# A two-layer trunk on one core: another order of the first stage, the embedding in two parts, and clipped differences on ScalarE

## Chip, core and metric

The kernel runs on one core of one Trainium2 chip. The metric is device microseconds from launch to end, the median of several executions. Engine names below: TensorE (PE, with PEld for its weight loads), VectorE (DVE), ScalarE (ACT), GpSimd (POOL), SyncE (SP).

## The reference

Two layers over a sequence of 512 rows of width 1024, all in fp32. Layer 0 mixes by a state-space scan (SSD, 8 groups of 4 heads, chunks of 128 rows), layer 1 by a gated MLP with a masked spatial product; each is followed by a SwiGLU FFN and a gated embedding.

```
for i in range(2):
    hn = rmsnorm(h, norm_mix[i])
    h = h + (ssd_mixer(hn, ...) if i % 2 == 0 else gmlp_mixer(hn, ...))
    h = h + swiglu(rmsnorm(h, norm_ffn[i]), ffn_w_gate[i], ffn_w_up[i], ffn_w_down[i])
    e = rmsnorm(p[i] @ ple_w_proj[i], ple_norm[i])
    gate = sigmoid(rmsnorm(h, ple_gate_norm[i]) @ ple_w_gate[i])
    h = h + gate * e
return rmsnorm(h, final_norm)
# inside the scan, per group and chunk:
lmat = exp(segsum(da))              # exp(cs[l] - cs[s]) where l >= s, else 0
y = einsum(C, B, lmat, x * dt) + C . previous states * exp(cs)
```

## The kernel before

The program holds the rows of `h` transposed, as 8 tiles `H[k]` of 128 features by 512 rows. Each weight arrives in raw tiles of 1 MB (two buffers) on SyncE's queue. A unit of 128x1024 is split in a high part `whi` (ScalarE, L88) and a low part `wlo` (VectorE, L89), three buffers each, and each product is three fp32r matmuls (`mm3`, L282 to L284): high by high, high by low, low by high. Activations are split likewise (`split`, L287 and L288).

The **first stage** (L663 to L728) is kept in the order of the code on every engine: sums of squares of the four row chunks of `x`, transposes, the row factors `rs0` (L421), scaled and split tiles of X (L426 to L430), and the products of the first two weight units (B and C of group 0). After it come two transposes of parameters (`to_columns`, L381), the product `wdt` · `H` (L737, 16 records) that gives dt, its copy (L738), and from it dt, the sums `cs` and their exponentials.

Everything after that is ordered by a scheduler that goes by code order and priorities; each engine then runs a fixed list. The **scan** of a group (`ssd(g)`) is a generator, advanced by `tock` while the projections of later groups run. It loads the rows of `cs` from DRAM (`csb`), takes clipped differences `min(cs[l] - cs[s], 0)` (L545, four per chunk) and their exponential (L546), forms `cb` (L585), its masked copy `cbm` (L587), `xdt` (L602), multiplies `csb` by `cbm` (L610, four), then states (L617) and outputs (L561, L563). Last come squares of the gated output `sq` and the group's statistic (`stat`: ScalarE's high part L287, VectorE's low part `rs` L288, matmuls L296 and L297, square root, reciprocal). The statistic of group g−1 falls among the steps of group g. There are two `sq` and two `rs` buffers.

After the last output projection stands the embedding of `p` (`ple_embed`, 48 matmuls), then the remainder of the output projection, each block of which is normalised (`nf.block`, L450 and L451), then the FFN. The FFN's own statistic keeps one `rs` buffer until the FFN ends. During it `spatial()` prepares the second layer: masked transposes `wsT`, and column sums, a fp32 matmul of `ones` with each (L935, 8 records), used by L938.

Of the kernel before, what the change touches and what calls it, by code (L numbers as in the profile page):

```python
# [43 lines left out]
class Weights:  # L44
# [16 lines left out]

    def _load(self, r):
        while self.loaded <= min(r, len(self.raws) - 1):
            raw = self.raw_pool.tile([P, 2048], F32, tag="wraw", name=f"wraw{self.loaded}")
            for dst, src in self.raws[self.loaded][0]:
                self.nc.sync.dma_start(out=dst(raw), in_=src)
            self.raws[self.loaded][1] = raw
            self.loaded += 1
# [33 lines left out]
def trunk(ctx: ExitStack, tc: tile.TileContext, x, p, norm_mix, norm_ffn, ssd_w_in, ssd_conv_w,  # L102
# [99 lines left out]
    add_proj(0)  # L202
    add_rows(ssd_w_out[0], 14, 2)
    add_ffn(0)
    for m in range(4):
# [32 lines left out]
    for c in range(NCH):  # L238
# [3 lines left out]
        x_tok.append((a, b))  # L242
    W._load(1)

# [87 lines left out]

    def ple_embed(i, spare):
        (ph, pl) = zip(*spare)
        E, accum = [], None
        for m2 in range(2):
            (wh, wl), = W.get()
            for mi in range(4):
                m = m2 * 4 + mi
                ps = bank()  # L340
                for k in range(2):
                    mm3(ps, wh[:, k, mi * P : (mi + 1) * P], wl[:, k, mi * P : (mi + 1) * P], ph[k], pl[k], k == 0, k == 1)
                e = slot(f"e{m}")
                nc.vector.tensor_scalar_mul(e, ps, pcol(80 + i * 8 + m))
                if accum is None:
                    accum = work("cbm")
                    act(accum, ps, AF.Square, scale=1.0 / 32)
                else:
                    sq = work("sq")
                    act(sq, ps, AF.Square, scale=1.0 / 32)  # L350
                    nc.gpsimd.tensor_tensor(accum, accum, sq, op=ALU.add)
                E.append(e)
# [6 lines left out]

        return E, finish()  # L360

# [40 lines left out]

    def x_rms(c):
        tt(ss[:, c : c + 1], ss2[:, c, 0:1], ss2[:, c, 1:2], op=ALU.add)
        act(rtok[:, c], ss[:, c : c + 1], AF.Sqrt, bias=eps6)
# [7 lines left out]

    rows = [None]

    def x_rows(c0, c1):
        if c0 == 0:
            rows[0] = bank()
        for c in range(c0, c1):
            tr(rows[0][:, c * P : (c + 1) * P], rtok[:, c].to_broadcast([P, P]))  # L420
        nc.vector.tensor_copy(rs0[:, c0 * P : c1 * P], rows[0][:, c0 * P : c1 * P])  # L421

# [103 lines left out]
    def ssd(g):  # L526
# [14 lines left out]
        def seg(c):  # L541

            for hh in range(4):
                o = lm[c][:, hh * P : (hh + 1) * P]
                nc.vector.tensor_scalar(o, o, cs[:, c, 4 * g + hh : 4 * g + hh + 1], 0.0, op0=ALU.subtract, op1=ALU.min)  # L545
            act(lm[c], lm[c], AF.Exp)  # L546

# [115 lines left out]
    with in_order(tc):  # L663
        warm(8)
        to_columns(3, rowN, 16)
        x_sums(0)
        x_transpose(0, 0, 6)
        x_sums(1)
        x_rms(0)
        x_transpose(1, 0, 6)  # L670
        x_sums(2)
        x_rms(1)
        x_transpose(2, 0, 6)
        x_sums(3)
        x_rms(2)
        x_rows(0, 3)
        x_transpose(3, 0, 6)
        x_rms(3)
        warm(2)
        x_rows(3, 4)  # L680
        warm(8)
        unit_hi(0)
# [4 lines left out]
        products(0, 0)  # L687
        x_lo(1, V_)
        products(0, 1)
        unit_hi(1)  # L690
# [24 lines left out]
        x_lo(7, G_)  # L715
        x_keep(3)
        W.taken = 2
        W._split(2)
        for k in range(4, KD):
            x_keep(k)  # L720
            products(0, k)
            products(1, k)
        nc.vector.tensor_copy(rowB[96:112].rearrange("b (h e) -> b h e", e=64),
                              d2[96:112].unsqueeze(2).to_broadcast([16, 2, 64]))
        to_columns(0, rowA, P)
        to_columns(1, rowB, P)

        tt(wdt, wdt, pcols[:, 3, :KD].unsqueeze(2).to_broadcast([P, KD, 32]), op=ALU.mult)  # L728
    for m in range(2):
        bc(m, first[m])  # L730
    dtT = work("csb")
    alog = dtT[:, :32]

    ps = bank()
    for k in range(2):
        for j in range(4):
            mm(ps[j * 32 : (j + 1) * 32], wdt[:, 2 * j + k], H[2 * j + k], start=k == 0, stop=k == 1)  # L737
    nc.vector.tensor_copy(dtT, ps)  # L738
    ps_dt = bank()
# [106 lines left out]
    while running:  # L846
        tick()
    E, finish_e = ple_embed(0, spare)
    assert not running


    nf = Norm(lambda k: pcol(16 + k))
    for m2 in range(2):
# [6 lines left out]
        for mi, ps in enumerate(pss):  # L860
            add_h(4 * m2 + mi, ps)
            nf.block(4 * m2 + mi)


# [57 lines left out]
    def spatial():  # L922
# [9 lines left out]
        yield  # L932
        for j in range(4):
            ps = bank()
            mm(ps, ones, wsT[j], start=True, stop=True)  # L935
            for gg in range(4):
# [127 lines left out]
    ffn(nf1, npg1.block, embed())  # L1064
    h_tok = [[slot(f"xh{2 * c + nt}") for nt in range(2)] for c in range(NCH)]

# [26 lines left out]
    def norm_out(c0, c1):  # L1093
        rms_tok(rtf, 1, c0, c1)
        for c in range(c0, c1):
            for n in range(2):
                o = slot(f"xl{2 * c + n}")
                if n and c == 3:
# [5 lines left out]
    for nt in range(2):  # L1104
# [19 lines left out]
        if nt == 0:  # L1124
            rtok2 = rstd_tok(npg1.accum)
            transpose_h(0)
            transpose_h(1)
        us = W.get(4 - first) if nt else []
# [41 lines left out]
```

## Time and profile before

| | |
|---|---|
| time, median of 3 | 1577.62 us (1577.13 to 1578.09) |
| the profiled execution | 1578.97 us |
| its span | 1577.0 us |
| mean granted TensorE clock | 0.997 |
| TensorE busy | 1553.9 us, 99% |
| VectorE, ScalarE, GpSimd busy | 904.9, 642.3, 285.7 us |

The span runs from the first to the last instruction; the execution's own time adds what lies around it. In the rows further down a record gives the start, the duration, the engine, the line, what it writes and reads, and in brackets how long the engine stood idle before it and what ended that.

### The profile page before, as it was taken

How to read it: one execution, taken by the hardware profiler on the slowest of the kernel's cores; microseconds unless marked ns; L12 is line 12 of the kernel's file. 1: busy time of each engine (PE TensorE's matmuls, PEld its weight loads, DVE VectorE, ACT ScalarE, POOL GpSimd, SP SyncE). 2: the span in 40 equal slices, each digit the busy share in tenths (PEclk: the TensorE clock that was granted, in tenths of full speed). 3: DMA queues.
4: the chain of work that ended last, by engine and by line, in shares of the span. 5: the costliest groups of instructions: out<-in, count | busy, mean ns of one | idle time of the engine just before them, and what ended most of it. 6: DMA issues, size and time to landing. Idle time of an engine off the chain costs nothing.

```text
span 1577.0 us, 18227 instructions
## 1 busy us (share of the span) xinstructions
PE 1553.9 (99%) x7350; PEld 1283.9 (81%) x7350; DVE 904.9 (57%) x1231; ACT 642.3 (41%) x842; POOL 285.7 (18%) x225
## 2 busy tenths in 40 slices
PE   7999999999999999999999999999999999999997
PEld 5887788888878788888888888888888888888886
DVE  6679895599886433433457647535544364433445
ACT  5456663466454222222344534323443242213336
POOL 3032220122254101100123200202221001101120
PEclk9999999999999999999999999999999999999999
DMA  5454443444424233233232333332232332322231
GB/s 168 118 128 127 128 127 106 125 114 110 140 81 133 88 99 107 81 107 100 75 120 81 107 94 100 99 108 80 81 120 85 103 106 81 107 96 91 80 107 54
DMA packets 151348, 164.15 MB, mean 104 GB/s; under 512 B 5320, under 2 KB 133856, under 8 KB 151264
## 3 DMA queue, kind: packets, MB, share of 16 engines
q1 hardware_dynamic: 149296, 157.62, 32.4%
q0 software_dynamic: 1760, 5.29, 1.2%
q8 instruction: 57, 0.93, 0.2%
q14 instruction: 27, 0.22, 0.0%
q10 hardware_dynamic: 208, 0.07, 0.0%
HBM read 160.75 MB, written 2.23 MB: 103 GB/s over the span
## 4 chain that ended last, share of the span: by engine, by line
PE 91%; DVE 5%; ACT 1%; DMA 1%; POOL 1%; issue 0%; ACTq 0%; DVEq 0%; POOLq 0%
PE ps L282 29%; PE ps L283 29%; PE ps L284 29%; PE ps L277 1%; DVE wlo L89 1%; PE ps L998 1%; PE ps L561 1%; DVE csb L545 1%; DVE csb L610 1%; PE ps L563 1%; DVE acc L485 1%; POOL sq L367 0%; PE ps L617 0%; DMA csb<-cs_dram 0%; DVE rs L300 0%
## 5 line engine op out<-in xcount | busy, mean ns | idle before, releaser
L88 ACT ACTIVATE whi<-wraw 128x1024 fp32r<-128x1024 f32 (+1 forms) x268 | 276.9, 1038 | 693.4 <-PE ps L283 612.2
L282 PE MATMUL ps<-xh,whi 128*128 128x512 f32 x1120 | 441.7, 394 | 0.1
L283 PE MATMUL ps<-xl,whi 128*128 128x512 f32 x1120 | 437.0, 390 | 1.5 <-DVE xl L451 0.9
L284 PE MATMUL ps<-xh,wlo 128*128 128x512 f32 x1120 | 437.0, 390 | 0.0
L89 DVE TENSOR_TENSOR wlo<-wraw,whi 128x1024 fp32r<-128x1024 f32 (+1 forms) x268 | 327.4, 1226 | 102.1 <-ACT whi L88 100.7
L282 PE MATMUL ps<-gh,whi 128*128 128x512 f32 x784 | 306.3, 391 | 0.0
L284 PE MATMUL ps<-gh,wlo 128*128 128x512 f32 x784 | 305.0, 389 | 0.0
L283 PE MATMUL ps<-gl,whi 128*128 128x512 f32 x784 | 305.0, 389 | 0.0
L282 PEld LDWEIGHTS ps<-xh,whi 128*128 128x128 f32 x1120 | 210.8, 188 | 47.9 <-issue 4.0
L283 PEld LDWEIGHTS ps<-xl,whi 128*128 128x128 f32 x1120 | 210.7, 188 | 45.7 <-DVE xl L451 1.4
L284 PEld LDWEIGHTS ps<-xh,wlo 128*128 128x128 f32 x1120 | 210.7, 188 | 44.3
L640 DVE TENSOR_TENSOR h<-h,ps 128x512 f32<-128x512 f32 x88 | 60.0, 685 | 196.8 <-PE ps L284 196.7
L878 POOL TENSOR_TENSOR zs<-zs,rs 128x512 f32<-128x512 f32 x44 | 73.8, 1680 | 544.2 <-ACT zs L877 544.2
L282 PEld LDWEIGHTS ps<-gh,whi 128*128 128x128 f32 x784 | 147.2, 188 | 30.7 <-issue 0.3
L284 PEld LDWEIGHTS ps<-gh,wlo 128*128 128x128 f32 x784 | 147.2, 188 | 30.5
L283 PEld LDWEIGHTS ps<-gl,whi 128*128 128x128 f32 x784 | 147.2, 188 | 30.1
L884 DVE TENSOR_TENSOR xsT<-ps,zs 128x512 f32<-128x512 f32 x44 | 30.4, 691 | 125.8 <-PE ps L284 117.1
L875 DVE TENSOR_TENSOR acc<-ps,rs 128x512 f32<-128x512 f32 x44 | 30.4, 690 | 108.5 <-PE ps L284 108.5
L367 POOL TENSOR_TENSOR sq<-sq,sq 128x512 f32<-128x512 f32 x43 | 68.4, 1590 | 129.8 <-ACT sq L364 127.8
L282 PE MATMUL ps<-whi,gh 128*128 128x512 f32 (+1 forms) x200 | 76.4, 382 | 0.0
L284 PE MATMUL ps<-whi,gl 128*128 128x512 f32 (+1 forms) x200 | 76.1, 381 | 0.0
L283 PE MATMUL ps<-wlo,gh 128*128 128x512 f32 (+1 forms) x200 | 76.1, 381 | 0.0
(301 smaller groups left out, 1426.3 us busy)
## 6 DMA issues: line engine op xcount, KB each, us to landing
wraw<-in_ffn_w_gate_dram SPq DMA_DIRECT2D x22, 1024.0 KB, 5.1
wraw<-in_ffn_w_up_dram SPq DMA_DIRECT2D x22, 1024.0 KB, 5.2
wraw<-in_ssd_w_in_dram SPq DMA_DIRECT2D x16, 1024.0 KB, 5.3
wraw<-in_ffn_w_down_dram SPq DMA_DIRECT2D x16, 1024.0 KB, 5.2
wraw<-in_gmlp_w_in_dram SPq DMA_DIRECT2D x16, 1024.0 KB, 5.5
wraw<-in_ssd_w_in_dram SPq DMA_DIRECT2D x16, 512.0 KB, 5.3
csb<-cs_dram SPq DMA_DIRECT2D x32, 256.0 KB, 4.7
wraw<-in_ple_w_gate_dram SPq DMA_DIRECT2D x8, 1024.0 KB, 5.2
```

The lines of the kernel that those rows point to most:

```text
L88: nc.scalar.activation(hi, src, AF.Copy)
L89: nc.vector.tensor_tensor(lo, src, f32(hi), op=ALU.subtract)
L277: nc.tensor.transpose(ps, src, ident)
L282: mm(ps, wh, xh, start=start, stop=False)
L283: mm(ps, wh, xl, start=False, stop=False)
L284: mm(ps, wl, xh, start=False, stop=stop)
L367: nc.gpsimd.tensor_tensor(sq, sq, accum, op=ALU.add)
L485: stt(a[:, d:], ps[:, : S - d], pcols[:, 0, j * 32 + b : j * 32 + b + 1], a[:, d:], op0=ALU.mult, op1=ALU.add)
L640: tt(H[m], H[m], ps, op=ALU.add)
L875: tt(a, ps, rs, op=ALU.mult)
L878: nc.gpsimd.tensor_tensor(s, s, rs, op=ALU.mult)
L884: tt(t, ps, gate[m], op=ALU.mult)
```

## The change

There are five parts. (1) In the first stage the four chunks are taken in a loop, the row factors are copied once, filler transposes stand between the chunks, and the second raw weight is issued from ScalarE's queue. The dt product follows the stage's products, ahead of the transposes of parameters, and its factor `wdt` is scaled before the splits. (2) The embedding is made in two halves, the second behind the last normalised block, and its unit of weights moves to the same place; the normalised X goes to the other set of slots. (3) The clipped differences are made by ScalarE, as Relu of `cs[s] - cs[l]`, and the exponential takes the negative. (4) The column sums are two fp32r matmuls per tile, of the low and the high part of `wsT`. (5) In the last stage half of the transposes of `h` move behind the first products of the second half.

```diff
@@ Weights
-    def _load(self, r):
+    def _load(self, r, queue=None):
...
-                self.nc.sync.dma_start(out=dst(raw), in_=src)
+                (queue or self.nc.sync).dma_start(out=dst(raw), in_=src)
@@ the list of weight units
     add_proj(0)
     add_rows(ssd_w_out[0], 14, 2)
+
+    W.units.append(W.units.pop(-3))
     add_ffn(0)
@@ loads at the start
-    W._load(1)
+    W._load(0)
@@ ple_embed
-        for m2 in range(2):
+
+        def half(m2):
+            nonlocal accum
             (wh, wl), = W.get()
...
-        return E, finish()
+        return E, half, finish()
@@ x_rows
-    def x_rows(c0, c1):
-        if c0 == 0:
-            rows[0] = bank()
-        for c in range(c0, c1):
-            tr(rows[0][:, c * P : (c + 1) * P], rtok[:, c].to_broadcast([P, P]))
-        nc.vector.tensor_copy(rs0[:, c0 * P : c1 * P], rows[0][:, c0 * P : c1 * P])
+    def x_rows(c):
+        if not rows:
+            rows.append(bank())
+        tr(rows[0][:, c * P : (c + 1) * P], rtok[:, c].to_broadcast([P, P]))
@@ ssd, seg(c)
-                nc.vector.tensor_scalar(o, o, cs[:, c, 4 * g + hh : 4 * g + hh + 1], 0.0, op0=ALU.subtract, op1=ALU.min)
-            act(lm[c], lm[c], AF.Exp)
+                act(o, o, AF.Relu, scale=-1.0, bias=cs[:, c, 4 * g + hh : 4 * g + hh + 1])
+            act(lm[c], lm[c], AF.Exp, scale=-1.0)
@@ the first stage
-        x_sums(0)
-        x_transpose(0, 0, 6)
...
-        x_rms(2)
-        x_rows(0, 3)
-        x_transpose(3, 0, 6)
+        for c in range(NCH):
+            x_sums(c)
+            if c:
+                x_rms(c - 1)
+            x_transpose(c, 0, 6)
+            if c:
+                x_rows(c - 1)
+            if c < 3:
+                warm(4)
         x_rms(3)
         warm(2)
-        x_rows(3, 4)
-        warm(8)
+        x_rows(3)
+        nc.vector.tensor_copy(rs0, rows[0])
+        warm(10)
...
         x_lo(1, V_)
+        W._load(1, nc.scalar)
         products(0, 1)
...
         x_keep(3)
+
+        tt(wdt, wdt, pcols[:, 3, :KD].unsqueeze(2).to_broadcast([P, KD, 32]), op=ALU.mult)
         W.taken = 2
         W._split(2)
...
             products(1, k)
+
+        ps = bank()
+        for k in range(2):
+            for j in range(4):
+                mm(ps[j * 32 : (j + 1) * 32], wdt[:, 2 * j + k], H[2 * j + k], start=k == 0, stop=k == 1)
+        dtT = work("csb")
...
         to_columns(1, rowB, P)
-
-        tt(wdt, wdt, pcols[:, 3, :KD].unsqueeze(2).to_broadcast([P, KD, 32]), op=ALU.mult)
+        nc.vector.tensor_copy(dtT, ps)
     for m in range(2):
         bc(m, first[m])
-    dtT = work("csb")
     alog = dtT[:, :32]
-
-    ps = bank()
-    for k in range(2):
-        for j in range(4):
-            mm(ps[j * 32 : (j + 1) * 32], wdt[:, 2 * j + k], H[2 * j + k], start=k == 0, stop=k == 1)
-    nc.vector.tensor_copy(dtT, ps)
@@ after the scan
-    E, finish_e = ple_embed(0, spare)
+    E, embed_half, finish_e = ple_embed(0, spare)
+    embed_half(0)
...
-    nf = Norm(lambda k: pcol(16 + k))
+    nf = Norm(lambda k: pcol(16 + k), swap=True)
...
             nf.block(4 * m2 + mi)
+    embed_half(1)
@@ spatial
         for j in range(4):
+            hi, lo = work("sq", F32R), work("rs", F32R)
+            split(wsT[j], hi, lo)
             ps = bank()
-            mm(ps, ones, wsT[j], start=True, stop=True)
+            mm(ps, ones_r, lo, start=True, stop=False)
+            mm(ps, ones_r, hi, start=False, stop=True)
@@ the last stage
-    h_tok = [[slot(f"xh{2 * c + nt}") for nt in range(2)] for c in range(NCH)]
+    h_tok = [[slot(f"{sets[1]}h{2 * c + nt}") for nt in range(2)] for c in range(NCH)]
...
-                o = slot(f"xl{2 * c + n}")
+                o = slot(f"{sets[1]}l{2 * c + n}")
...
             transpose_h(0)
+        if nt:
             transpose_h(1)
```

The line numbers of the changed kernel are higher: mm3 is L284 to L286, `split` L289 and L290, `stat`'s matmuls L298 and L299, Relu and Exp L549 and L550, `cbm` L591, `xdt` L606, L610 becomes L614, the dt product L732 and the column sums L942 and L943.

On TensorE, at the end of the first stage, the list of before has the last product, two transposes of parameters (from `Btok` and `cbm`) and the dt product:

```order
L283 MATMUL ps_257<-xl_61_323,whi_252 128x512
L284 MATMUL ps_257<-xh_60_322,wlo_253 128x512
L381 MATMUL ps_369<-ident,Btok_93 128x128
L381 MATMUL ps_372<-ident,cbm_94 128x128
L737 MATMUL ps_391<-h_45_274,u_127 32x512
L737 MATMUL ps_391<-h_55_314,u_127 32x512
L737 MATMUL ps_391<-h_63_336,u_127 32x512
```

In the changed kernel the same place reads:

```order
L285 MATMUL ps_270<-xl_61_336,whi_265 128x512
L286 MATMUL ps_270<-xh_60_335,wlo_266 128x512
L732 MATMUL ps_382<-h_45_287,u_125 32x512
L732 MATMUL ps_382<-h_55_327,u_125 32x512
L732 MATMUL ps_382<-h_63_350,u_125 32x512
...
L732 MATMUL ps_382<-h_64_358,u_125 32x512
L732 MATMUL ps_382<-h_66_374,u_125 32x512
L386 MATMUL ps_393<-ident,Btok_93 128x128
L386 MATMUL ps_396<-ident,cbm_94 128x128
L284 MATMUL ps_429<-xh_33_246,whi_346 128x512
```

The dt product has moved ahead of the two transposes, and the next projection follows them.

On VectorE, in group 4 of the scan, before (`rs_2161` is the low part of group 3's statistic, `cbm_2101` belongs to group 4):

```order
L89 TENSOR_TENSOR wlo_2013<-wraw_1849,whi_2012 128x1024
L288 TENSOR_TENSOR rs_2161<-sq_1983,sq_2160 128x512
L89 TENSOR_TENSOR wlo_2060<-wraw_1953,whi_2059 128x1024
L587 TENSOR_TENSOR cbm_2101<-ps_2096,U 128x512
L610 TENSOR_TENSOR csb_2017<-csb_2017,cbm_2101 128x512
L602 TENSOR_TENSOR xdt_2115<-ps_2110,dt 128x512
L602 TENSOR_TENSOR xdt_2122<-ps_2117,dt 128x512
L610 TENSOR_TENSOR csb_2019<-csb_2019,cbm_2101 128x512
L610 TENSOR_TENSOR csb_2023<-csb_2023,cbm_2101 128x512
L610 TENSOR_TENSOR csb_2027<-csb_2027,cbm_2101 128x512
```

In the changed kernel, same place (`rs_2174` and `cbm_2114`):

```order
L89 TENSOR_TENSOR wlo_2026<-wraw_1862,whi_2025 128x1024
L89 TENSOR_TENSOR wlo_2073<-wraw_1966,whi_2072 128x1024
L591 TENSOR_TENSOR cbm_2114<-ps_2109,U 128x512
L614 TENSOR_TENSOR csb_2030<-csb_2030,cbm_2114 128x512
L606 TENSOR_TENSOR xdt_2128<-ps_2123,dt 128x512
L606 TENSOR_TENSOR xdt_2135<-ps_2130,dt 128x512
L614 TENSOR_TENSOR csb_2032<-csb_2032,cbm_2114 128x512
L614 TENSOR_TENSOR csb_2036<-csb_2036,cbm_2114 128x512
L614 TENSOR_TENSOR csb_2040<-csb_2040,cbm_2114 128x512
L290 TENSOR_TENSOR rs_2174<-sq_1996,sq_2173 128x512
```

The low part of the statistic has moved from ahead of `cbm` to behind the last product of `csb` and `cbm`. Groups 3, 5 and 6 read alike.

On TensorE the column sums of the changed kernel stand in one piece, where before there were four L935:

```order
L942 MATMUL ps_4516<-rs_4513,ones_r 128x512
L943 MATMUL ps_4516<-sq_4512,ones_r 128x512
L942 MATMUL ps_4527<-rs_4524,ones_r 128x512
L943 MATMUL ps_4527<-sq_4523,ones_r 128x512
L942 MATMUL ps_4538<-rs_4535,ones_r 128x512
L943 MATMUL ps_4538<-sq_4534,ones_r 128x512
L942 MATMUL ps_4549<-rs_4546,ones_r 128x512
L943 MATMUL ps_4549<-sq_4545,ones_r 128x512
```

On VectorE, around them, before:

```order
L884 TENSOR_TENSOR xsT_4493<-ps_4468,zs_4424 128x512
L89 TENSOR_TENSOR wlo_4534<-wraw_4427,whi_4533 128x1024
L288 TENSOR_TENSOR gl_624_4496<-xsT_4493,gh_623_4495 128x512
L938 SCALAR_TENSOR_TENSOR prev_4005<-ps_4499,pcols,prev_4005 128x128 x4
L938 SCALAR_TENSOR_TENSOR CT_4006<-ps_4505,pcols,CT_4006 128x128 x4
L938 SCALAR_TENSOR_TENSOR csb_4007<-ps_4511,pcols,csb_4007 128x128 x4
L938 SCALAR_TENSOR_TENSOR csb_4008<-ps_4517,pcols,csb_4008 128x128 x4
```

And in the changed kernel (`rs_4524`, `rs_4535` and `rs_4546` are the low parts of the second to the fourth tile; the first stands ten rows further up):

```order
L889 TENSOR_TENSOR xsT_4506<-ps_4481,zs_4437 128x512
L946 SCALAR_TENSOR_TENSOR prev_4018<-ps_4516,pcols,prev_4018 128x128
L89 TENSOR_TENSOR wlo_4567<-wraw_4440,whi_4566 128x1024
L290 TENSOR_TENSOR xl_624_4509<-xsT_4506,xh_623_4508 128x512
L946 SCALAR_TENSOR_TENSOR prev_4018<-ps_4516,pcols,prev_4018 128x128 x3
L290 TENSOR_TENSOR rs_4524<-csb_4023,sq_4523 128x512
L290 TENSOR_TENSOR rs_4535<-cbm_4024,sq_4534 128x512
L946 SCALAR_TENSOR_TENSOR CT_4019<-ps_4527,pcols,CT_4019 128x128 x4
L946 SCALAR_TENSOR_TENSOR csb_4020<-ps_4538,pcols,csb_4020 128x128 x4
L290 TENSOR_TENSOR rs_4546<-Btok_4025,sq_4545 128x512
L946 SCALAR_TENSOR_TENSOR csb_4021<-ps_4549,pcols,csb_4021 128x128 x4
```

The low parts stand between the L946 that read the sums (L938 before), behind the split of a weight unit.

## Rows read from the trace of the kernel before

**Rows 1.** The page: span, and busy time of TensorE.

```profile
span 1577.0 us, 18227 instructions
...
PE 1553.9 (99%) x7350; PEld 1283.9 (81%) x7350; DVE 904.9 (57%) x1231; ACT 642.3 (41%) x842; POOL 285.7 (18%) x225
```

**Rows 2.** Waits of TensorE: us in total, times, longest.

```profile
PE ps L737 <- DVE u L728: 3.3, 1, 3.3
PE ps L296 <- DVE rs L288: 1.8, 2, 1.4
...
PE ps L617 <- POOL xdd L605: 0.7, 1, 0.7
```

**Rows 3.** Timeline of the first stage, VectorE and TensorE: start, us, what.

```profile
12.35 0.56 DVE L421 COPY rs<-ps 128x384 f32<-128x384 f32 x1 [0.57 <-PE ps L277]
...
14.59 1.41 DVE L426 SCALAR_TENSOR_TENSOR e<-ps,pcols,rs 128x512 f32<-128x512 f32 x2
...
18.04 0.63 PE L284 MATMUL ps<-xh,wlo 128*128 128x512 f32 x1
...
20.60 0.56 PE L284 MATMUL ps<-xh,wlo 128*128 128x512 f32 x1
```

**Rows 4.** Timeline of TensorE, end of the first stage.

```profile
30.56 0.39 PE L284 MATMUL ps<-xh,wlo 128*128 128x512 f32 x1
...
34.45 3.56 PE L737 MATMUL ps<-h,u 128*32 128x512 f32 x16 [3.29 <-DVE u L728]
37.95 0.51 PE L282 MATMUL ps<-xh,whi 128*128 128x512 f32 x1
```

**Rows 5.** Windows after that wait: busy by engine, PEclk, DMA share, GB/s.

```profile
35.00:36.00 1.00, 1.00 (x8) 0.27 (x4) 1.00 (x2) 0.52 (x1) 0.00 (x0) 0.50 1.15 345
```

**Rows 6.** Timeline of TensorE where the first FFN starts.

```profile
465.53 0.39 PE L284 MATMUL ps<-xh,wlo 128*128 128x512 f32 x1
465.76 0.39 PE L282 MATMUL ps<-xh,whi 128*128 128x512 f32 x1
467.08 0.50 PE L283 MATMUL ps<-xl,whi 128*128 128x512 f32 x1 [0.93 <-DVE xl L451]
```

**Rows 7.** Groups by line and shape, 84 to 440 us, VectorE and ScalarE.

```profile
L545 DVE TENSOR_SCALAR csb<-csb,cs 128x128 f32<-128x128 f32 x112 | 36.9, 391 | 7.4 <-DMA csb<-cs_dram 7.4
...
L546 ACT ACT_TABLE_LOAD x14 | 18.0, 1283 | 3.9 <-DMA csb<-cs_dram 2.9 <-DVE csb L545 0.8
```

**Rows 8.** Timeline of ScalarE, activations of 128x128.

```profile
63.37 0.27 ACT L793 ACTIVATE dec<-ps 128x128 f32<-128x128 f32 x1
```

**Rows 9.** Windows, one group of the scan: busy by engine, PEclk, DMA.

```profile
200.00:240.00 40.00, 39.45 (x223) 32.56 (x222) 38.51 (x61) 26.25 (x33) 8.42 (x8) 1.00 0.43 126
```

**Rows 10.** Timeline of TensorE, cb of group 4, statistic of group 3.

```profile
230.99 1.05 PE L585 MATMUL ps<-CT,BT 128*128 128x128 f32 x8
...
235.96 0.40 PE L296 MATMUL ps<-rs,ones_r 128*128 128x512 f32 x1
```

**Rows 11.** Timeline of VectorE, same place.

```profile
229.47 0.69 DVE L288 TENSOR_TENSOR rs<-sq,sq 128x512 fp32r<-128x512 f32 x1 [0.63 <-ACT sq L287]
...
232.07 0.69 DVE L587 TENSOR_TENSOR cbm<-ps,U 128x512 f32<-128x512 f32 x1 [0.43 <-PE ps L585]
```

**Rows 12.** Timeline of group 2, VectorE and TensorE.

```profile
152.89 0.68 DVE L587 TENSOR_TENSOR cbm<-ps,U 128x512 f32<-128x512 f32 x1
...
158.94 0.47 PE L296 MATMUL ps<-rs,ones_r 128*128 128x512 f32 x1 [1.39 <-DVE rs L288]
```

**Rows 13.** Timeline of the column sums, TensorE and VectorE.

```profile
527.53 1.88 PE L935 MATMUL ps<-csb,ones 128*128 128x512 f32 x4
...
531.19 0.39 PE L283 MATMUL ps<-xl,whi 128*128 128x512 f32 x1
...
528.64 1.23 DVE L89 TENSOR_TENSOR wlo<-wraw,whi 128x1024 fp32r<-128x1024 f32 x1
...
530.38 1.12 DVE L938 SCALAR_TENSOR_TENSOR prev<-ps,pcols,prev 128x128 f32<-128x128 f32 x4
```

More of the change, by code (lines that the diff above doesn't have):

```diff
@@ L412, in x_transpose @@
             tr(xT[k][:, c * P : (c + 1) * P], x_tok[c][k // 4][:, (k % 4) * P : (k % 4 + 1) * P])
-    rows = [None]
-    def x_rows(c0, c1):
-        if c0 == 0:
-            rows[0] = bank()
-        for c in range(c0, c1):
-            tr(rows[0][:, c * P : (c + 1) * P], rtok[:, c].to_broadcast([P, P]))
-        nc.vector.tensor_copy(rs0[:, c0 * P : c1 * P], rows[0][:, c0 * P : c1 * P])
+    rows = []
+    def x_rows(c):
+        if not rows:
+            rows.append(bank())
+        tr(rows[0][:, c * P : (c + 1) * P], rtok[:, c].to_broadcast([P, P]))
     def x_scale(k):
@@ L665, in trunk @@
         to_columns(3, rowN, 16)
-        x_sums(0)
-        x_transpose(0, 0, 6)
[L668 to L674, printed above, removed]
-        x_rms(2)
-        x_rows(0, 3)
-        x_transpose(3, 0, 6)
+        for c in range(NCH):
[7 more added lines that the diff above has]
+                warm(4)
         x_rms(3)
         warm(2)
-        x_rows(3, 4)
-        warm(8)
+        x_rows(3)
+        nc.vector.tensor_copy(rs0, rows[0])
+        warm(10)
         unit_hi(0)
```

## The prediction

> **What bounds the kernel now.** Read the page first: TensorE is busy for 1553.9 of 1577.0 us [rows 1], so the program is one long row of matmuls and its end moves only by what opens or closes a gap in that row. The other engines' totals matter only where TensorE waits for them. Next the waits of TensorE [rows 2]: one of 3.3 us for the `u` of L728 and short ones, 1.8 us in two at L296 and 0.7 us at L617. All the time that any edit could win is in such gaps and in matmuls that run slowly, some 20 us; what it can lose has no such bound, since the matmul order is fixed and one late operand holds up everything behind it. So I went through the order of the changed kernel and asked, at each place where it differs, when the operand of the next matmul is ready. The profiled execution took 1578.97 us, 1.97 us around the span; the runs' median is 1577.62. I make the sum on the span and carry it over to the median. A measurement here tells about 0.2% (3.2 us) from no change.
>
> **First stage.** Before, the fourth chunk's sum stands on VectorE behind a copy of 0.56 us, and the first scaling starts at 14.59 [rows 3]. Afterwards there is one copy at the end. The sum comes about 0.5 us earlier, and the shorter chain of copies may give another 0.4: I take 0.9, bounds 0 and 0.9. The six steps from 18.04 to 20.60 take 0.43 us each [rows 3], where the step later is 0.23 (465.53 to 465.76) [rows 6]: eight such matmuls lose about 1.6 us. The added filler transposes keep TensorE going ahead of them, so these may run at the faster pace; the scaling and splitting on VectorE and ScalarE then hold back part, so I take 1.1, bounds 0 and 1.6. Products end 2.0 us earlier (0 to 2.5), at about 28.8 instead of 30.8. The next weight load goes out on ScalarE's queue; the place of that issue costs ScalarE under half a microsecond before copies that aren't waited for.
>
> **dt matmul.** Before, the last product is issued at 30.56, L737 starts at 34.45 and the next projection at 37.95 [rows 4]. Its 16 records cost 3.5 us because after the wait the granted clock is 0.50 [rows 5], 1.2 GHz instead of 2.4. Its factor `u` is now multiplied ahead of the splits, and the matmul follows the products directly: no wait, and 16 records at full clock, 1.75 us. Products at 28.8, dt to 30.55, two transposes to 30.8: the projection starts 7.1 us earlier. New is a wait behind it: the transposes of dtT now come after 8 matmuls (before, after 17), at 30.8+1.8=32.6, and the copy of dtT stands on VectorE behind two splits of 1.2 us each and two small copies. I put 0.8 us on that (0 to 1.5). **First stage and dt: +6.3 us** (4.0 to 8.0).
>
> **Embedding in two halves.** Where the FFN starts, L283 starts at 467.08 where 465.99 was due, 1.1 us lost [rows 6], and L296 waits 0.4 more (the smaller of the two in [rows 2]). Both wait for the normalisation blocks of `h`. Afterwards 24 matmuls of the second half, 24 × 0.23 = 5.5 us, stand between those blocks and the FFN, more than the 1.5 us that is late. **+1.5 us** (0.8 to 1.8). The same weights are only taken in another order, and the slots of X change name; I cost both at nothing, since splits there run ahead by a buffer.
>
> **Relu on ScalarE.** VectorE loses 112 instructions, 36.9 us in 84 to 440 [rows 7] (128 in all). ScalarE gains 128 and 14 table loads of 1.28 us [rows 7]. No Relu is in the trace; the nearest row is an activation of 128x128 at 0.27 us [rows 8], so 16 of a group cost at most 4.3 us. In 200 to 240, one group, ScalarE is busy 26.25 of 40 us [rows 9]; with 4.3 and two more loads, 2.6, it is at 33.2. It doesn't bind by its sum, and VectorE, 38.51 of 40 [rows 9], gets relief: the 0.7 us at L617 [rows 2], where VectorE's `xdt` was late, goes. **+0.9 us** with the restart (0 to 1.0).
>
> The Trainium skill ("ScalarE: Activation LUTs", Rules for kernel authors) says to put relu on VectorE, not ScalarE; and its section What ACT_TABLE_LOAD costs gives 280 ns + 0.833 ns per element with a pointer bias, less 93 ns of overlap, an estimate of 0.29 us for 128. The activation row (0.27) is near that, and by that rule the sum would be the same unless ScalarE is late, which the last rival prices.
>
> What costs is the order that comes with it. L296 of group g−1 stands on TensorE 4.97 us after L585 of group g (230.99 and 235.96) [rows 10]; the matmuls between the two are the same in groups 3 to 6. Its operand is `rs` of L288. Before, L288 ran at 229.47, ahead of `cbm` at 232.07 [rows 11]. In the changed order L288 stands behind `cbm`, two `xdt` and four L610. How long that takes is seen in group 2 of before, where the order already is so: from `cbm` at 152.89 to L296 at 158.94, 6.05 us, and TensorE waits 1.39 us [rows 12]. Now `cbm` begins 1.08 us after L585 [rows 10, 11]. So L296 comes 7.13 us after L585 where 4.97 was free: 2.16 us of wait in each of four groups, 8.6 us. Group 7 moves its statistic by only three matmuls; I put 1.3 on it (0 to 2.5). Group 2 keeps what it has. VectorE is emptier, but the chain starts at L585, a matmul, so relief elsewhere doesn't bring it forward. **−9.9 us** (0, if the order's chain is shorter than in group 2 by all of the 2.16, to −16, if the last Exp is late by another microsecond in each).
>
> **Column sums by split halves (L935).** Before, four matmuls in 8 records run from 527.53 and the next projection's second matmul is at 531.19 [rows 13], so with a step of 0.23 for the first they take 3.4 us. Eight fp32r matmuls at the step of 0.23 [rows 6] are 1.8: 1.6 us less, were the operands there. But all low halves share one `rs` buffer (the FFN's own statistic keeps the other), so each split waits for the matmul that read the one before. VectorE's queue from 527.53 on: `xsT`, one L946, the split L89 from 528.64 on for 1.23 [rows 13], `xl`, three L946 (0.28 each, by the 1.12 of four [rows 13]), then the second low half. A split of 512 columns costs the 0.69 of L288 [rows 11]. That is 528.64+1.23+0.69+0.84+0.69 = 532.1; its matmul, 0.3; the third low half to 533.1; four L946, 1.1, and four more, 1.1, that wait for the third pair; the fourth low half to 536.0; the last pair, and the projection at 536.6 instead of 531.0. −5.6 us, bounds +1.6 (no wait) and −6; the first gap, over 4 us, is longer than the 3.3 that halved the clock at 34.45 [rows 2, 5], so 0.9 more (0 to 1.7), half of what the slow clock cost there. **−6.5 us** (+1.6 to −7.7).
>
> **Tail.** Half of the transposes of `h` move behind the first products of the second half. No row speaks for a gain: **−0.3 us** (+0.3 to −0.7).
>
> Sum: 6.3 + 1.5 + 0.9 − 9.9 − 6.5 − 0.3 = −8.0 us. 1577.6 + 8.0 = **1585.6 us**, slower by 0.5%.
>
> **The rivals.** (a) *Nothing new waits*, the other side. Queues have room and both chains fit: 6.3+1.5+0.9+1.6−0.3 = +10.0, 1567.6 us. For it: VectorE is unloaded. Against it: group 2 [rows 12] and the single `rs` buffer. The point that decides is whether L288 is done 4.97 us after L585. Chance 0.16. (b) *Only the column sums wait*: 8.4 − 6.5 = +1.9, 1575.7, the same within the measurement. 0.14. (c) *Only the groups wait*: 8.4+1.6−9.9 = +0.1, 1577.5. 0.10. (d) *ScalarE is the new bound in the groups*: Relus at the full 0.27 and loads between them make the last Exp and L287 late by another 1.1 us in each of five groups, and the clock falls in the gap of the sums: −8.0−5.5−1.2, 1592.3 and up to 1598. For it: 33.2 of 40 busy, in an order that alternates table sets. Against it: the last Exp has 3 us until its L610. 0.13. My forecast, both wait, has 0.47, its own range 1581 to 1591.
>
> **How the numbers follow.** Slower by over 0.2%: the forecast's 0.47 less 0.03 at its lower end, and (d): 0.57, and 0.02 from upper ends of (b) and (c): 0.59. Faster by over 0.2%: (a) and 0.04 of (b) and (c): 0.20. The rest, 0.21, is the same. The range 1569 to 1595 leaves out most of (a) and the end of (d), under 0.2 together.
>
> **What the profile would show.** Right: no wait for L728's successor and dt matmuls right after the products at clock 1.00; no wait for L451 at the FFN's start; waits of some 2 us "PE L296 <- DVE L288" (new numbers 298 and 290) in five or six groups; a wait of over 3 us at the `ones_r` matmuls near 520. Wrong: if L288's operand comes within 5 us of L585, or low halves don't queue for one buffer, the time falls to (c), (b) or (a); if ScalarE's Exp ends those waits, it is (d).

## The result and the profile after

The changed kernel is slower: 1598.65 us median of 4 runs (1594.44 to 1601.05) beside 1577.86 us for the kernel before in the same runs. The ratio is 1.0128, 95% interval 1.0114 to 1.0142, 20.8 us where I forecast 8, and above my range. From here on times of different chips are compared by their ratio to the kernel before on the same chip.

The page of the changed kernel, against [rows 1]:

```profile
span 1598.7 us, 18261 instructions
...
PE 1559.3 (98%) x7364; PEld 1288.4 (81%) x7364; DVE 870.6 (54%) x1106; ACT 699.5 (44%) x988; POOL 282.1 (18%) x225
```

VectorE is 34 us less busy and ScalarE 57 us more; TensorE's own busy time grew by 5 us. The waits of TensorE, against [rows 2]:

```profile
PE ps L298 <- DVE rs L290: 15.1, 5, 4.0
PE ps L942 <- DVE rs L290: 6.3, 3, 3.8
PE ps L279 <- ACT xsT L490: 2.0, 1, 2.0
```

The wait of 3.3 us for `u` and that for `xdd` are gone. In their place the statistic's matmul waits 15.1 us in five groups, the column sums 6.3, and group 7's transposes 2.0 for `xsT`.

Where the time went is read from the starts of the same matmul in both traces. The table gives start after minus start before (L585 and L589 for `cb`, L617 and L621 for the states, L308 and L310 for the factor ahead of the second layer); each is a difference of two records of TensorE, in us. A column stands for one execution, so it can differ from the medians: both_undone ends at −11.35 here, and its median is 7.3 us under before.

| | after | diff_dve | both_undone | best | low_early | fill |
|---|---|---|---|---|---|---|
| cb of group 0 | −7.32 | −6.65 | −6.58 | −7.32 | −5.84 | −7.59 |
| cb of group 2 | −8.45 | −6.69 | −7.71 | −7.72 | −5.65 | −6.99 |
| cb of group 3 | −3.49 | −7.16 | −9.32 | −7.41 | −5.20 | −4.78 |
| cb of group 4 | −2.42 | −7.06 | −9.55 | −7.44 | −6.35 | −2.16 |
| cb of group 5 | 2.52 | −7.08 | −9.60 | −7.44 | −4.80 | 4.21 |
| cb of group 6 | 8.59 | −7.07 | −9.59 | −7.43 | −4.80 | 7.34 |
| cb of group 7 | 13.46 | −7.08 | −9.60 | −7.44 | −4.80 | 10.63 |
| states of group 7 | 15.64 | −7.08 | −9.60 | −7.44 | −2.51 | 14.32 |
| factor of layer 2 | 21.71 | −1.07 | −11.34 | −10.72 | 3.84 | 24.26 |
| last matmul | 21.71 | −1.06 | −11.35 | −10.73 | 3.82 | 24.24 |

Read the first column from the top, in steps. In the changed kernel 7.3 us are won by the first stage and 1.1 in group 1. The groups then lose 24.4 us (−8.45 to 15.98 at the last group's own statistic, 437.04 beside 421.06). The FFN's start wins 1.7 (to 14.25 at the column sums, 541.78 beside 527.53), the sums lose 7.5, and the last stage changes nothing.

The first stage, VectorE's first scaling and TensorE, against [rows 3, 4]:

```profile
12.81 1.41 DVE L430 SCALAR_TENSOR_TENSOR e<-ps,pcols,rs 128x512 f32<-128x512 f32 x2
...
16.33 0.40 PE L286 MATMUL ps<-xh,wlo 128*128 128x512 f32 x1
16.56 0.40 PE L284 MATMUL ps<-xh,whi 128*128 128x512 f32 x1
...
28.32 0.39 PE L286 MATMUL ps<-xh,wlo 128*128 128x512 f32 x1
28.64 1.92 PE L732 MATMUL ps<-h,u 128*32 128x512 f32 x16
...
30.69 0.48 PE L284 MATMUL ps<-xh,whi 128*128 128x512 f32 x1
```

The scaling starts 1.8 us earlier, the products run at 0.23 us from the start, the last is issued at 28.32 instead of 30.56, and the dt product follows at once. The next projection starts at 30.69 instead of 37.95.

Group 5, TensorE: `cb`, and the statistic of group 4 (against [rows 10, 12]):

```profile
317.80 1.05 PE L589 MATMUL ps<-CT,BT 128*128 128x128 f32 x8
...
325.88 0.79 PE L298 MATMUL ps<-rs,ones_r 128*128 128x512 f32 x1 [2.95 <-DVE rs L290]
```

VectorE in the same place: a weight split, `cbm`, and the statistic's low half.

```profile
318.78 1.22 DVE L89 TENSOR_TENSOR wlo<-wraw,whi 128x1024 fp32r<-128x1024 f32 x1 [3.31 <-ACT whi L88]
319.92 0.69 DVE L591 TENSOR_TENSOR cbm<-ps,U 128x512 f32<-128x512 f32 x1
...
322.45 2.78 DVE L614 TENSOR_TENSOR csb<-csb,cbm 128x512 f32<-128x512 f32 x3
325.15 0.68 DVE L290 TENSOR_TENSOR rs<-sq,sq 128x512 fp32r<-128x512 f32 x1
```

And ScalarE: four Relus, a table load, an exponential, the high part of a weight, and further on the high half of the statistic. The fence below it has the same half in group 5 of before.

```profile
314.59 1.27 ACT L549 ACTIVATE csb<-csb,cs 128x128 f32<-128x128 f32 x4
315.87 1.28 ACT L550 ACT_TABLE_LOAD   x1
317.17 0.63 ACT L550 ACTIVATE csb<-csb 128x512 f32<-128x512 f32 x1
317.70 1.04 ACT L88 ACTIVATE whi<-wraw 128x1024 fp32r<-128x1024 f32 x1
...
323.86 0.61 ACT L289 ACTIVATE sq<-sq 128x512 fp32r<-128x512 f32 x1
```

```profile
315.67 0.62 ACT L287 ACTIVATE sq<-sq 128x512 fp32r<-128x512 f32 x1
```

Read them backwards. The matmul at 325.88 waited 2.95 us for the low half of 325.15. That stood 5.2 us behind `cbm`, as in group 2 of before. But `cbm` itself starts 2.1 us after `cb`, not 1.08 [rows 10, 11]: it stands behind the split at 318.78, and that idled 3.31 us for ScalarE, which came to the weight's high part only at 317.70, behind Relu, load and exponential. Groups 4 and 6 read the same (`cbm` 2.3 and 2.2 us after `cb`); in group 3 it is 1.1.

One thing more stands in these rows. The high half of the statistic, which the low half is made from, has slid on ScalarE as well: in group 5 of before it started 0.4 us behind `cb` (315.67 beside 315.28), here 6.1 us. It ends at 324.47, and TensorE was idle from 322.93 on. So VectorE's order is what held the low half last. But had VectorE been free, the low half would still have come 0.68 us after 324.47, and 2.2 of the 2.95 us of wait would have stayed, by an estimate from these rows.

Then the clock: windows of the same place, PEclk third from the end.

```profile
305.00:328.00 23.00, 20.05 (x95) 16.56 (x94) 15.28 (x20) 22.83 (x35) 7.20 (x6) 0.94 0.26 87
328.00:329.00 1.00, 1.00 (x3) 0.74 (x3) 1.00 (x2) 0.09 (x1) 0.00 (x0) 0.50 0.69 141
331.00:332.00 1.00, 1.00 (x3) 0.73 (x3) 1.00 (x2) 0.00 (x0) 0.00 (x0) 0.50 1.01 251
332.00:333.00 1.00, 1.00 (x6) 0.81 (x5) 0.89 (x2) 0.00 (x0) 0.00 (x0) 0.98 0.05 13
```

From 305 to 328 ScalarE is busy 22.83 of 23 us. Behind the wait TensorE runs at 0.50, 1.2 GHz, from 326 to 332 and so makes half the matmuls. By the same differences, taken from the statistic to the next `cb`, that costs 3.0 us in this group (5.63 to 8.59) and 2.3, 1.6 and 1.7 in groups 2, 4 and 6: 8.6 in all.

The column sums, TensorE and VectorE, against [rows 13]:

```profile
541.78 0.40 PE L942 MATMUL ps<-rs,ones_r 128*128 128x512 f32 x1
...
546.25 0.47 PE L942 MATMUL ps<-rs,ones_r 128*128 128x512 f32 x1 [3.85 <-DVE rs L290]
...
547.50 0.80 PE L942 MATMUL ps<-rs,ones_r 128*128 128x512 f32 x1 [0.55 <-DVE rs L290]
...
550.64 0.76 PE L942 MATMUL ps<-rs,ones_r 128*128 128x512 f32 x1 [1.91 <-DVE rs L290]
...
551.63 0.63 PE L284 MATMUL ps<-gh,whi 128*128 128x512 f32 x1
...
545.42 0.68 DVE L290 TENSOR_TENSOR rs<-csb,sq 128x512 fp32r<-128x512 f32 x1
...
549.81 0.68 DVE L290 TENSOR_TENSOR rs<-Btok,sq 128x512 fp32r<-128x512 f32 x1
```

The pairs come at 541.8, 546.2, 547.5 and 550.6, the last three each behind its low half, and the next projection at 551.6. The granted clock behind the first wait:

```profile
548.00:553.00 5.00, 3.09 (x8) 1.92 (x8) 3.34 (x11) 0.00 (x0) 0.00 (x0) 0.50 0.00 0
```

### The profile page after: what moved, and what is told of

Its sections match the earlier page's. It is cut to its first block, busy times and chain, and to the rows that moved or that the text cites. A ratio compares the mean times of both kernels' runs of the same rounds, so it can differ in the third digit from the quotient of the medians.

```text
span 1598.7 us, 18261 instructions
## 1 busy us (share of the span) xinstructions
PE 1559.3 (98%) x7364; PEld 1288.4 (81%) x7364; DVE 870.6 (54%) x1106; ACT 699.5 (44%) x988; POOL 282.1 (18%) x225
## 4 chain that ended last, share of the span: by engine, by line
PE 85%; ACT 7%; DVE 3%; DMA 3%; issue 1%; ACTq 0%; SPq 0%; DVEq 0%
PE ps L284 27%; PE ps L285 27%; PE ps L286 27%; DMA csb<-cs_dram 2%; ACT L550 1%; ACT csb L549 1%; ACT whi L88 1%; DVE csb L614 1%; PE ps L1006 1%; ACT csb L550 1%; ACT L490 1%; PE ps L621 1%; PE ps L279 1%; PE ps L565 1%; DVE wlo L89 0%
## 5 line engine op out<-in xcount | busy, mean ns | idle before, releaser
L284 PE MATMUL ps<-xh,whi 128*128 128x512 f32 x1056 | 419.0, 397 | 1.1 <-ACT xh L431 1.1
L285 PE MATMUL ps<-xl,whi 128*128 128x512 f32 x1056 | 413.4, 392 | 1.6 <-DVE xl L434 1.6
L286 PE MATMUL ps<-xh,wlo 128*128 128x512 f32 x1056 | 413.4, 391 | 0.0
L284 PE MATMUL ps<-gh,whi 128*128 128x512 f32 x848 | 330.8, 391 | 0.0
L285 PE MATMUL ps<-gl,whi 128*128 128x512 f32 x848 | 330.1, 390 | 0.0
L286 PE MATMUL ps<-gh,wlo 128*128 128x512 f32 x848 | 330.1, 390 | 0.0
L284 PEld LDWEIGHTS ps<-xh,whi 128*128 128x128 f32 x1056 | 200.0, 189 | 44.2 <-issue 1.9
L286 PEld LDWEIGHTS ps<-xh,wlo 128*128 128x128 f32 x1056 | 199.6, 189 | 42.4 <-POOL wlo L659 0.3
L284 PEld LDWEIGHTS ps<-gh,whi 128*128 128x128 f32 x848 | 159.5, 188 | 33.7 <-ACT gh L289 0.4
L286 PEld LDWEIGHTS ps<-gh,wlo 128*128 128x128 f32 x848 | 159.5, 188 | 33.4 <-DVE wlo L89 0.3
L284 PE MATMUL ps<-whi,xh 128*128 128x512 f32 (+1 forms) x200 | 76.4, 382 | 0.0
L286 PE MATMUL ps<-whi,xl 128*128 128x512 f32 (+1 forms) x200 | 76.2, 381 | 0.0
L285 PE MATMUL ps<-wlo,xh 128*128 128x512 f32 (+1 forms) x200 | 76.1, 381 | 0.0
```

The costliest lines, as they stand in the source:

```text
L284: mm(ps, wh, xh, start=start, stop=False)
L285: mm(ps, wh, xl, start=False, stop=False)
L286: mm(ps, wl, xh, start=False, stop=stop)
```

## The experiments

**diff_dve: the differences back on VectorE.**

```diff
-                act(o, o, AF.Relu, scale=-1.0, bias=cs[...])
-            act(lm[c], lm[c], AF.Exp, scale=-1.0)
+                nc.vector.tensor_scalar(o, o, cs[...], 0.0, op0=ALU.subtract, op1=ALU.min)
+            act(lm[c], lm[c], AF.Exp)
```

> The changed kernel with the clipped differences back on VectorE, all else kept. Theory (the groups' loss of some 24 us comes from the Relu on ScalarE, through the order and the late ScalarE behind it): the waits of the statistic's matmul on its low half fall from 15.1 us in five groups to 2 us or less, the clock stays at 1.00 in the groups, and the time is 1574 to 1578. Rival (the loss comes from the other parts, such as the earlier start of the groups): the waits stay over 8 us and the time is over 1588.

Measured: 1577.55 us, ratio 1.0011 (1.0001 to 1.0020). Its waits:

```profile
PE ps L942 <- DVE rs L290: 6.3, 3, 3.8
...
PE ps L298 <- DVE rs L290: 0.9, 1, 0.9
```

The groups lose nothing any more (−6.69 to −7.08 in the table), and the wait at the sums stays as it was. The Relu is what brings the groups' loss.

**sums_fp32: the column sums back to fp32.**

```diff
-            mm(ps, ones_r, lo, start=True, stop=False)
-            mm(ps, ones_r, hi, start=False, stop=True)
+            mm(ps, ones, wsT[j], start=True, stop=True)
```

> The changed kernel with the column sums back as fp32 matmuls of ones, all else kept. Theory (the single rs buffer makes the four pairs wait): 7.5 us are won back, the time is 1590 to 1592, nothing else moves. Rival (the waits there only stand in for waits that come later in the FFN): under 3 us are won, the time is over 1595.

Measured: 1592.70 us, ratio 1.0106 (1.0091 to 1.0121), on its chip 16.7 us over before instead of 20.8. That is 4.1 won, between the two expectations, but kernels that have the groups' waits scatter by 3 to 7 us from run to run. The trace is sharper: from the start of the FFN to the second layer it loses 0.0 us against before, where the changed kernel loses 7.5, as the theory said.

**both_undone: both of these.**

> The changed kernel without the Relu and without the split column sums: the new first stage, the embedding in halves and the moved transposes alone. Theory (the first stage wins 7.3 us and the embedding 1.7): 1567 to 1570, the first projection starts 7.3 us earlier than before, no wait on the normalised X where the FFN starts. Rival (the gains are given back in the groups, which then find their weights or loads late): 1573 or more.

Measured: 1568.73 us, ratio 0.9955 (0.9940 to 0.9970), 8.8 us under diff_dve on the same chip. Of the difference of their traces, 10.3 us, the split sums have 7.7, between the FFN's start and the second layer. The groups have 2.5, and there the order of every engine is the same in both: they are scatter between executions. No wait over 0.6 us is left behind the first stage, where the FFN starts neither:

```profile
PE ps L279 <- ACT rt L312: 0.6, 1, 0.6
PE ps L567 <- DVE prev L622: 0.6, 1, 0.6
```

The first stage, the embedding in halves and the moved transposes are worth 7 us together, and nothing gives them back.

**low_early: only the two halves of the statistic's split earlier,** the high one on ScalarE and the low one on VectorE. The order of TensorE is the changed kernel's but for a few products, and for group 6's statistic, which stands three matmuls earlier in group 7.

```diff
+        with tc.high_priority(offset=400 if tag == "sq" else 0):
-        split(accum, hi, lo)
+            split(accum, hi, lo)
```

> The changed kernel with a higher priority for the two splits of the group's statistic alone: the low half stands ahead of the masked copy or right behind it on VectorE, the order of the matmuls on TensorE is that of the changed kernel, the Relu stays on ScalarE, the column sums stay as they are. Theory A (the order on VectorE is the cause in groups 3 to 6, ScalarE only in groups 2 and 7): no waits on the low half in groups 3 to 6, 2 to 6 us lost in groups 2 and 7 at operands from ScalarE, ratio to before 1.002 to 1.006. Theory B (ScalarE is late everywhere): waits of 1 us or more in at least four groups, ratio over 1.009.

Measured: 1581.93 us, ratio 1.0026 (1.0015 to 1.0036): 16 of the 20 us are back with the Relu still on ScalarE. The waits that count:

```profile
PE ps L943 <- DVE rs L290: 6.1, 3, 3.8
PE ps L279 <- ACT xsT L491: 2.1, 1, 2.1
PE ps L622 <- ACT Btok L598: 1.8, 1, 1.8
...
PE ps L284 <- ACT gh L289: 1.4, 1, 1.4
```

No statistic waits any more, and the table stands at −5.20 in group 3 and at −4.80 from group 5 on. What is left of ScalarE is 1.8 us for `Btok` in group 2, 1.4 for `gh` in group 4, which no theory had, and 2.1 for `xsT` in group 7. Theory A holds in that the order is the cause in groups 3 to 6, not the load. It is the order of both engines, though: the edit moves both halves, so how much the low half alone would give back is not shown.

**stat_early: the whole statistic earlier, its matmuls too.** Here `stat` itself stands under the higher priority.

> The changed kernel with the group's statistic scheduled with a higher priority: its low half stands ahead of the masked copy and the four products on VectorE again, and its matmul some 3.5 us earlier on TensorE. The Relu stays on ScalarE. Theory A (the order on VectorE is the cause): the waits on the low half fall under 4 us in sum, the time is 1578 to 1584. Theory B (ScalarE is late, the order only shows it): waits of 8 us or more stay, at this matmul or at the next that needs ScalarE (states, outputs), and the time is over 1588.

Measured: 1590.99 us, ratio 1.0098 (1.0082 to 1.0115).

```profile
PE ps L943 <- DVE rs L290: 6.1, 3, 3.8
PE ps L621 <- ACT Btok L597: 4.5, 1, 4.5
```

The waits on the low half are gone as A said, and from group 3 to group 7 the starts of `cb` lose no more (−1.75 to −0.05 by the same differences), yet the time is B's. With the matmuls the square root and the reciprocal (3.3 us on VectorE) moved ahead of the products as well, and in group 2 the states then wait 4.5 us for `Btok`: that group loses 5.2 us, the column sums 8.7. It moved matmuls and splits together; low_early, which moves the splits alone, decides.

**fill: 16 filler transposes ahead of each statistic's matmul.**

```diff
+        if tag == "sq":
+            for _ in range(16):
+                tr(ps[:, :P], ident)
         mm(ps, ones_r, lo, start=True, stop=False)
```

> The changed kernel with 16 filler transposes on TensorE directly ahead of each group statistic's matmul (16 x 0.11 = 1.8 us of work that is done inside the wait; the order on VectorE and ScalarE is unchanged). Theory (of the groups' 24 us some 8.6 us are matmuls at half clock behind a wait of 3 us, the rest the waits themselves): the waits shrink to 1 to 2.5 us behind the fillers, the clock stays at 1.00, and the time is 6 to 9 us under the changed kernel, a ratio to before of 1.007 to 1.009. Rival (the slow stretch behind a wait comes from late operands, not from the clock): under 2 us are won, ratio over 1.011.

Measured: 1602.61 us, ratio 1.0160 (1.0141 to 1.0179): 5 us slower, where both sides expected less time. Group 5 again, TensorE, and a window behind it, then a window of group 4:

```profile
324.47 1.91 PE L279 MATMUL ps<-ident 128*128 128x128 f32 x16
327.51 0.50 PE L301 MATMUL ps<-rs,ones_r 128*128 128x512 f32 x1 [1.14 <-DVE rs L290]
...
329.00:330.00 1.00, 1.00 (x6) 0.84 (x5) 0.96 (x2) 0.71 (x2) 0.00 (x0) 1.00 0.21 48
...
240.00:242.00 2.00, 2.00 (x6) 1.52 (x6) 1.93 (x4) 0.81 (x2) 0.00 (x0) 0.50 0.50 142
```

In groups 5 and 6 the mechanism is there: the fillers take 1.9 us of the wait, the clock stays at 1.00, and by the table they lose 3.1 and 3.3 us instead of 6.1 and 4.9. But three of the eight statistics didn't wait and pay for their fillers, one in group 1 (1.7 us by the table) and two in group 7, which loses 7.1 us instead of 2.5 up to its own statistic. What group 2 wins, groups 3 and 4 give back (11.2 us over the three, 11.0 without fillers): in group 4 TensorE still waits 2.9 us and the clock falls to 0.50. The 8.6 us of slow clock can't be taken off the loss by themselves.

**sums_pairs: the split sums two tiles at a time.**

```diff
+        for j0 in (0, 2):
+            halves = []
+            for j in (j0, j0 + 1):
+                halves.append((work("sq", F32R), work("u", F32R)))
+                split(wsT[j], *halves[-1])
+            yield
+            for j in (j0, j0 + 1):
...
```

> The changed kernel with the column sums still as fp32r matmuls, but two tiles at a time: both splits are made one step ahead, the low halves in the two u buffers, which are free there, and the matmuls a step later. Theory (only the one rs buffer and the split right ahead of its matmul make the pairs wait): no wait at these matmuls, 9 us won on the changed kernel (7.5 of wait and clock, 1.6 of faster matmuls), ratio to before 1.006 to 1.008. Rival (VectorE and ScalarE have no room for the splits there): waits of 2 us or more stay, or come at the next matmuls, and under 6 us are won.

Measured: 1590.22 us, ratio 1.0082 (1.0063 to 1.0101), 13.0 us over before instead of 20.8. Its waits:

```profile
PE ps L298 <- DVE rs L290: 14.3, 5, 3.3
PE ps L279 <- ACT xsT L490: 2.1, 1, 2.1
```

There is none at the sums, and from the FFN's start to the second layer the trace wins 1.55 us on before where the changed kernel loses 7.5: the 9 us of the theory. The cause was the shared buffer together with the split right ahead of its matmul; the edit takes away both, so their shares are not shown.

**best: sums_pairs with the differences on VectorE.**

> The new first stage, the embedding in halves, the moved transposes and the column sums two tiles at a time, with the clipped differences on VectorE. Theory (the parts add): 1.6 us under the kernel without Relu and split sums, a ratio to before of 0.9935 to 0.9955. Rival (the split sums cost their gain elsewhere): 0.9955 or more.

Measured: 1568.05 us, ratio 0.9939 (0.9927 to 0.9952), the fastest kernel here. The interval overlaps that of both_undone, so the times leave 1.6 us for the faster sums open. The traces do not: from the FFN's start to the second layer all five kernels with these sums win 1.55 us on before, and both with fp32 sums win nothing.

**no_diff: no differences at all.**

```diff
-                act(o, o, AF.Relu, scale=-1.0, bias=cs[...])
-            act(lm[c], lm[c], AF.Exp, scale=-1.0)
+                pass
+            act(lm[c], lm[c], AF.Exp)
```

> The changed kernel without any clipped differences: neither engine makes them, the exponential is taken of the loaded rows as they are (this part of the computation is left out). It bounds what any other place for this work could win. Theory (TensorE had no gap in the groups that this work caused, apart from about 1 us in group 1 and 1 us in group 2): against the kernel that has the differences on VectorE and the split sums (1.6 us over before) it wins 0 to 2 us. Rival (the work on VectorE costs TensorE time in each group): it wins 5 us or more.

The kernel leaves out this part of the computation. Measured: 1577.05 us in one run, 0.2 us under before; diff_dve stands 1.6 us over before. In the traces `cb` of group 7 starts 10.3 us earlier than before, with the differences on VectorE 7.1 to 9.6 (diff_dve, best, both_undone). Wherever this work goes, there were some 1 to 3 us to win; one run gives no more than that.

**best_low: best with the early splits.**

> The kernel with the differences on VectorE and the column sums two tiles at a time, and the same higher priority for the splits of the group's statistic. Theory (the 1.7 us wait on the low half in group 2 goes, nothing else moves): ratio to before 0.992 to 0.994, no wait over 1 us from 80 to 1500 us. Rival (the earlier splits push other work of VectorE, which is at 38 of 40 us there, behind TensorE's need): 0.995 or more.

Measured: 1568.89 us, ratio 0.9946 (0.9933 to 0.9958), no gain.

```profile
PE ps L284 <- ACT gh L289: 2.1, 2, 1.3
PE ps L622 <- POOL x L611: 1.6, 1, 1.6
```

The wait at group 2's statistic is gone; others, at GpSimd and at `gh`, took its place. That is the rival's mechanism in part, since `gh` comes from ScalarE; the ratio lies between the two expectations.

**no_fill: best without fillers in the first stage.**

> The kernel with the differences on VectorE and the column sums two tiles at a time, without filler transposes in the first stage. Theory (the fillers keep TensorE at full clock for the first products): the first eight or more products run at 0.43 us instead of 0.23, the first stage ends 1 to 2 us later, ratio 0.001 above the same kernel with fillers. Rival (the clock is up anyway once the products start): no change of step, first stage as early as with fillers or earlier.

Measured: 1568.97 us, ratio 0.9943 (0.9929 to 0.9956). TensorE's first products and the last:

```profile
16.39 0.63 PE L286 MATMUL ps<-xh,wlo 128*128 128x512 f32 x1
...
18.95 0.59 PE L286 MATMUL ps<-xh,wlo 128*128 128x512 f32 x1
...
28.94 0.39 PE L286 MATMUL ps<-xh,wlo 128*128 128x512 f32 x1
```

Six steps take 2.56 us, 0.43 each, as before; the last product is issued at 28.94 instead of 28.32. So the theory's mechanism shows, but it gives 0.6 us, not 1 to 2, and traces with the fillers differ by more than that among themselves (−5.84 to −7.59 in the table's first row). In the time nothing shows.

**relu_mended: low_early with sums_pairs.**

> The changed kernel, the Relu on ScalarE kept, with both things mended that cost it most: the splits of the group's statistic early, and the column sums two tiles at a time. Theory (what is left of the Relu's price is ScalarE's lateness in groups 2 and 7, 4 to 6 us): ratio to before 0.996 to 0.999, 2 to 8 us over the same kernel with the differences on VectorE. Rival (with the order mended the Relu is free, since VectorE gets relief): 0.993 to 0.995, no more than that kernel.

Measured: 1572.71 us, ratio 0.9961 (0.9947 to 0.9975).

```profile
PE ps L279 <- ACT xsT L491: 2.6, 1, 2.6
PE ps L622 <- ACT Btok L598: 1.6, 1, 1.6
...
PE ps L284 <- ACT gh L289: 1.4, 1, 1.4
```

The Relu with a mended order beats the kernel before. The same kernel with the differences on VectorE is best_low: relu_mended stands 0.0015 above it, some 2.4 us, and 0.0022 above best, and the intervals overlap with both. So a gain of the Relu isn't seen, and a price of 2 to 4 us is likely but not settled. The three waits shown are all for ScalarE.

## Why the prediction was wrong

The sign and the two places were right, the size was not: 20.8 us against 8.0.

*First stage and dt, +6.3.* Measured +7.3. The scaling came 1.8 us earlier, not 0.9; the fillers' share was smaller than the 1.1 I gave them (0.6 by no_fill); the new wait of 0.8 us behind dt did not come (matmuls run on from 30.69).

*Embedding, +1.5.* Measured 1.7. *Tail, −0.3.* Measured 0.

*Relu's relief in group 1, +0.9.* Measured 1.1, but not by the mechanism, as far as the runs show: both_undone, without the Relu, wins the same 1.1, and low_early, with it, has a wait of 0.9 for `xdd`. The wait comes and goes between executions, so the figure was luck.

*Column sums, −6.5.* Measured −7.5 in the trace: the chain through one buffer took 9.85 us from the first pair to the next projection (541.78 to 551.63), 9.1 by my walk, with part of it at half clock.

*Groups, −9.9: the step that failed.* Measured −24.4, past the bound of −16. It failed in three terms: a wait put at nothing, a wait taken too small, and a clock cost left out. The sentence "Group 2 keeps what it has" was wrong: there ScalarE was late and the loss grew by 2.65 us. "So L296 comes 7.13 us after L585" put 2.16 us on each of groups 3 to 6, and the waits lost 2.0 in group 3 and 3.1 to 3.3 in groups 4 to 6: there `cbm` did not start 1.08 us behind `cb`, because the weight split ahead of it waited for ScalarE. I walked VectorE's queue alone. (In group 3 of before the low half stood right behind `cbm` and not ahead of it, as I had read it; the products of `csb` and `cbm` came behind it all the same.) Rival (d) had ScalarE late, but at the last exponential and at the statistic's high half; that half did come late, at 324.47 in group 5, yet VectorE's chain came later still. And the slow clock behind a wait, which I priced at the dt product and at the sums, I left out here: 8.6 us. Group 7 lost 2.5, not 1.3, and not at its statistic but at `xsT`, from ScalarE. Together 2.65 + 11.6 + 8.6 + 2.5 − 1.0, the last a short wait of before that fell away in group 3.

Rival (d) gave 1592 to 1598 for a late ScalarE; the result is just past its far end, and low_early shows that most of it is not that engine's load: with the load unchanged and the two halves of each group's statistic earlier, 16 us come back.

Of the price of a Relu I took at most 0.27 us from [rows 8]. In the trace of the changed kernel:

```profile
L549 ACT ACTIVATE csb<-csb,cs 128x128 f32<-128x128 f32 x116 | 37.5, 391 | 22.7 <-DMA csb<-cs_dram 22.6 <-PE ps L567 0.2
```

The records are 391 ns and four follow each other in 1.28 us (306.98 to 308.26), 0.32 each. The Trainium skill ("ScalarE: Activation LUTs", What ACT_TABLE_LOAD costs) states 280 ns and 0.833 ns per column for a pointer bias, and 93 ns of overlap back to back: for 128 columns an estimate of 387 ns, and of 0.29 us back to back. The trace bears it out better than my row of an activation without such a bias. The Trainium skill ("ScalarE: Activation LUTs", Rules for kernel authors) advises to leave relu to VectorE, with a gain per element in bf16 as its reason. The runs agree in the outcome, since diff_dve stands 0.0117 under the changed kernel, but not by that reason: a record of VectorE takes 391 ns too [rows 7], and it is the order that costs.

Still open: how the 16 us divide between the order of VectorE and that of ScalarE, and why the stretch at half clock goes on for 6 us behind the wait in group 5 and for 3 in groups 4 and 6.

## What to carry to other kernels

Moving work from the busier engine to the idler one is worth what the bounding engine waited for it, here some 1 to 3 us, whatever the busy times say. Such a move rewrites the order on every engine. Look in the new order for what the bounding engine waits on next, walk back through every engine that makes it, and pull those instructions forward. Splits that share one buffer and feed consecutive matmuls make a chain; give each its own buffer and a step of lead.

## What the hardware showed

In the changed kernel waits of 2.0 us in groups 3 and 7 left the granted clock at 1.00; waits of 2.95 to 4.0 us in groups 2 and 4 to 6 were followed by 3 to 6 us at 0.50, a loss of 1.6 to 3.0 us each. The length of the wait alone doesn't tell which: in fill and in sums_pairs the waits of 1.9 and 2.1 us for `xsT` in group 7 were followed by 3.4 us at 0.50. The kernel with these waits also scatters: 1594.4 to 1601.1 us in four runs, where before stays within 1577.1 to 1579.2.
